# A transformer block in float32: the order of the down projection, where its weight sums are made, and the order of the up projection's matmuls

## The chip, the cores and the metric

The kernel runs on one core of one Trainium2 chip. The metric is the device time of one execution, in microseconds (us). Engines: TensorE (PE, with its weight loads as PEld), VectorE (DVE), ScalarE (ACT), GpSimd (POOL) and SyncE (SP, which here issues most loads). Each engine has a list of instructions of its own, in the order that the program gives; between engines semaphores decide.

## The reference

One block over 256 rows of 2048 columns: three kinds of attention, gates, an output product, and then the part that the change touches, a gated feed-forward layer with a short convolution.

```python
def reference(x, mem, ..., g_ffn, w_up, conv_w, conv_b, w_down):
    ...
        x = x + merged @ w_out[l]

        h2 = rms_norm(x, g_ffn[l])
        u = causal_depthwise_conv(h2 @ w_up[l], conv_w[l], conv_b[l])
        u_gate, u_val = jnp.split(u, 2, axis=-1)
        x = x + (jax.nn.silu(u_gate) * u_val) @ w_down[l]
    return x
```

`w_up` is 2048 x 11264, `w_down` 5632 x 2048.

## The kernel before

Products in float32 are made of parts. A piece of weights (128 partitions x 1024 columns, 512 KB) is loaded into `raw`; ACT rounds it to `hi`, DVE makes `lo = raw - hi`. The activations are kept as such parts too, and a product is two or three matmuls: in the down stage always three (`three`, L898): hi by hi, hi by the activation's lo, lo by hi. So each piece costs a load, one ACT and one DVE instruction ahead of its matmuls. `hi` and `lo` have four buffers each. `raw` has four in one pool and four more (`more`) in a pool that opens in the down stage; from the seventh load on they alternate (`buffer`, L874).

**Up stage** (L794 on). For 11 blocks of four row tiles of `u` and both halves (gate and value), 22 groups in all, it goes over eight pieces of `w_up`. Each piece holds two k tiles by four row tiles, and for each of these eight PE makes one long matmul (512 columns, L811: the weights' hi with both parts of the activations) and one short one (256 columns, L812: the weights' lo with the hi part). Long and short alternate. At five of the 22 groups (`BEATS`) a matmul of 32 columns on zeros goes ahead (L800). After each group the convolution (`conv`, L730) of its two row pairs follows on ACT and DVE: a copy `cr` out of PSUM, an add, a multiplication `u`, taps `y` and `z` on ACT with adds on DVE, and in the second half the product and its parts `aT`.

Beside it the up stage makes sums of down weights (`weight_sums`, L760): it loads four blocks of `w_down` into `r`, adds them on DVE and stores them by POOL's queue in DRAM tiles `T`, for the first half of the output columns in two stores, for the second half in one.

**Down stage** (L823 on). The output is made in two halves of 1024 columns, each in 22 products over two k tiles. `PLANS` has a letter for each. An `e` (`eight`, L911) takes two pieces and 24 long matmuls into four banks `X`. An `s` (`seven`, L926) gets the same result from seven block products, 21 matmuls, by sums of weight blocks (`t13`, `t42`) and sums of activation blocks (`forms`, L849), into `X` and four more banks `Y`, which `gather` (L954) adds up later. In the first half both sums of an `s` are loaded from `T`; in the second half `t13` is made here by two adds on DVE (L937, L938). The forms of product p are written some products ahead.

In this stage the instructions are written in a plain order, and the scheduler is free to move those of SP, ACT and DVE, by its own estimate of when things are due. Only instructions given to `keep_in_program_order` stay as written; in the down stage none are.

Of the kernel before, what the change touches and what calls it, by code (L numbers as in the profile page):

```python
# [44 lines left out]
def hybrid_block(  # L45
# [714 lines left out]
    def weight_sums(nb, p):  # L760
        n0 = nb * PIECE
        r = cps[2].tile([P, 2, 2, 512], F32, tag="r", name=f"r_{nb}_{p}")
        for j, n in ((0, 1), (0, 0), (1, 1), (1, 0)):
            tc.keep_in_program_order(
                nc.sync.dma_start(r[:, j, n], dv[:, 2 * p + j, n0 + n * 512 : n0 + (n + 1) * 512])
            )
            yield 1
        yield 1
        b01 = r[:, 0, 1]
        tc.keep_in_program_order(nc.vector.tensor_tensor(r[:, 0, 0], r[:, 0, 0], b01, ALU.add))  # L770
        if nb == 0:
# [4 lines left out]
        T = dram.tile([P, 2, 1024], F32, name=f"T_{nb}_{p}")  # L776
        made[nb, p] = T
        for h in range(nb, 2):
            yield 2
            nc.gpsimd.dma_start(T[:, h], r[:, h].rearrange("p b n -> p (b n)"))  # L780

# [12 lines left out]
    for f0 in range(0, FT, 4):  # L794
        for s in range(2):
            pairs = [two_banks(f"u{f0 + i}_{s}") for i in (0, 2)]
            c0 = s * D_FF + f0 * P
            if f0 // 2 + s in BEATS:
                tc.keep_in_program_order(
                    nc.tensor.matmul(pairs[0][:, 0, :32], lhsT=idle[:, :P], rhs=idle[:, :32], start=True, stop=True)  # L800
                )
            if asked and f0 // 2 + s > 0:
                adding.append([weight_sums(*asked.pop(0)), 0])
            for k in range(0, KT, 2):
                hi, lo = piece(upv[:, k : k + 2, c0 : c0 + 512], 2, 512, f"u{f0}_{s}_{k}")
                for j in range(2):
                    first, last = k + j == 0, k + j == KT - 1
                    for i in range(4):
                        c = slice(i * P, (i + 1) * P)
                        ps = pairs[i // 2][:, i % 2]  # L810
                        nc.tensor.matmul(ps, lhsT=hi[:, j, c], rhs=hT[:, k + j, :], start=first, stop=False)  # L811
                        nc.tensor.matmul(ps[:, :S], lhsT=lo[:, j, c], rhs=hT[:, k + j, :S], start=False, stop=last)  # L812
                add_on()
                tick()
# [16 lines left out]

    ov = out[0].rearrange("(t p) d -> p t d", p=P)
# [16 lines left out]
    def forms(p):  # L849
# [8 lines left out]
        nc.vector.tensor_tensor(  # L858
            d, two, v[:, 0, :, 1].unsqueeze(1).to_broadcast([P, 2, 2, P]), ALU.subtract
        )  # L860
        nc.vector.tensor_tensor(g, v[:, :, 0, 0], v[:, :, 1, 0], ALU.add)
        nc.vector.tensor_tensor(r[:, :2], d[:, :, 0], d[:, :, 1], ALU.add)
        nc.vector.scalar_tensor_tensor(r[:, FS2], r[:, FS1], -1.0, g[:, 0], ALU.mult, ALU.subtract)
        nc.vector.tensor_tensor(r[:, FS4], r[:, FS2], g[:, 1], ALU.add)
        to = sf[:, p] if p < 10 else form_of(p, slice(0, 3))
        last = form_of(p, FS4)
        nc.scalar.copy(to[:, :, 0], r[:, :3])
        nc.scalar.copy(last[:, 0], r[:, FS4])
        nc.vector.tensor_tensor(to[:, :, 1], r[:, :3], to[:, :, 0].bitcast(F32), ALU.subtract)
        nc.vector.tensor_tensor(last[:, 1], r[:, FS4], last[:, 0].bitcast(F32), ALU.subtract)  # L870
# [14 lines left out]
    def load_sums(T, h, name):  # L885
        t = buffer(f"raw_t{h}_{name}")
        nc.sync.dma_start(t, T[:, h])
        return t

    def parts(src, name):  # L890
# [3 lines left out]
        nc.scalar.copy(hi[:, :n], src)  # L894
        nc.vector.tensor_tensor(lo[:, :n], src, hi[:, :n].bitcast(F32), ALU.subtract)  # L895
# [14 lines left out]

    def eight(p, n0, X, first, last):  # L911
        w = []
        for k in (2 * p, 2 * p + 1):
            w.append(parts(load(k, n0), f"d{n0}_{k}"))
            if not last:
                for t in range(NT):
                    for n in range(2):
                        three(X[t][n], *a_of(k, t), w[-1][n], first and k == 2 * p)
            tick()
        if last:  # L920
            for t in range(NT):
                for n in range(2):
                    for j in range(2):
                        three(X[t][n], *a_of(2 * p + j, t), w[j][n], last=j == 1)

    def seven(p, n0, X, Y, first, last):  # L926
        k0, k1 = 2 * p, 2 * p + 1
        T = made[n0 // PIECE, p]
        full = n0 > 0
        raw0, raw1 = load(k0, n0, PIECE if full else 512), load(k1, n0)  # L930
        t13 = buffer(f"t13_{n0}_{p}") if full else load_sums(T, 0, f"{n0}_{p}")
        t42 = load_sums(T, 1, f"{n0}_{p}")
        (B00,) = parts(raw0[:, :512], f"d{n0}_{k0}")
        three(Y[0], *a_of(k0, 0), B00, first, last)
        B10, B11 = parts(raw1, f"d{n0}_{k1}")
        if full:
            nc.vector.tensor_tensor(t13[:, :512], raw0[:, :512], raw0[:, 512:], ALU.add)  # L937
            nc.vector.tensor_tensor(t13[:, 512:], raw0[:, 512:], raw1[:, 512:], ALU.add)  # L938
        three(X[0][0], *a_of(k1, 0), B10)
        three(X[0][1], *f_of(p, FS4), B11)  # L940
        tick()
        T1, T3 = parts(t13, f"t13_{n0}_{p}")
        three(Y[2], *f_of(p, FS1), T1, first, last)
        three(Y[3], *f_of(p, FS3), T3, first, last)
        T4, T2 = parts(t42, f"t42_{n0}_{p}")
        three(Y[1], *f_of(p, FS2), T2, first, last)
        three(X[1][0], *a_of(k1, 1), T4)
        tick()

    def gather(n0, Y):  # L950

        yield 3
        xr = lambda t, n: xrows[t, n]
        e, f = (sm.tile([P, 512], F32, tag="junk", bufs=2, name=f"{c}_{n0}") for c in "ef")  # L954
        nc.scalar.copy(e, Y[0])
        nc.vector.tensor_tensor(xr(0, 0), xr(0, 0), Y[0], ALU.add)
        nc.vector.tensor_tensor(e, e, Y[1], ALU.add)
        yield
        nc.vector.tensor_tensor(f, e, Y[2], ALU.add)
        nc.vector.tensor_tensor(e, e, Y[3], ALU.add)  # L960
        nc.vector.tensor_tensor(xr(0, 1), xr(0, 1), f, ALU.subtract)
        yield
        nc.vector.tensor_tensor(xr(1, 0), xr(1, 0), e, ALU.add)
        nc.vector.tensor_tensor(e, e, Y[2], ALU.add)
        nc.vector.tensor_tensor(xr(1, 1), xr(1, 1), e, ALU.subtract)

    formed = 0
    for nb, plan in enumerate(PLANS):
        n0 = nb * PIECE
        xrows = {}  # L970
        banks = [two_banks(f"d{nb}_{i}") for i in range(4)]
        if nb:
            banks = banks[2:] + banks[:2]
        X = [[banks[t][:, n] for n in range(2)] for t in range(NT)]
        Y = [banks[2 + i // 2][:, i % 2] for i in range(4)]
        ns, s = plan.count("s"), 0
        straight = list(range(FT // 2 - 1, ns - 1, -1)) if nb else list(range(ns, FT // 2))
        done = []
        for i, c in enumerate(plan):
            if c == "s":  # L980
                seven(s, n0, X, Y, s == 0, s == ns - 1)
                s += 1
                if s == ns:
                    later(gather(n0, Y))
            else:
                p = straight.pop(0)
                eight(p, n0, X, i == 0, i == len(plan) - 1)
                done.append(p)
                if len(done) == 4:
                    for t in range(NT):  # L990
                        for n in range(2):
                            xrows[t, n] = down_pool().tile([P, 512], F32, tag="xr", name=f"xr_{nb}_{t}_{n}")
                            nc.gpsimd.dma_start(xrows[t, n], xkeep[2 * nb + n][:, t])
                if formed < NSEVEN[0] and len(done) >= 2 or nb and formed < ns and len(done) > 1:
                    forms(formed)
                    formed += 1
        assert s == ns and not straight
        finish()
        for t in range(NT):
            for n in range(2):  # L1000
                o = sm.tile([P, 512], F32, tag="junk", bufs=2, name=f"o_{nb}_{t}_{n}")
                parts_ = 2 if (nb, t, n) == (1, 1, 1) else 1
                for i in range(parts_):
                    w = 512 // parts_
                    oc = slice(i * w, (i + 1) * w)
                    xc = slice(n0 + n * 512 + i * w, n0 + n * 512 + (i + 1) * w)
                    nc.vector.tensor_tensor(o[:, oc], xrows[t, n][:, oc], X[t][n][:, oc], ALU.add)
                    nc.scalar.dma_start(ov[:, t, xc], o[:, oc])

# [30 lines left out]
```

## Time and profile before

| | us |
|---|---|
| median of three runs (1508.73 to 1511.41) | 1509.15 |
| the profiled execution | 1509.21 |
| its span, first to last instruction | 1507.5 |
| L812, 1408 short matmuls of the up stage: busy, mean ns of one | 395.6, 281 |
| lo parts of `d` pieces, 128x1024, down stage (68): mean ns | 1219 |
| hi parts of the same: mean ns | 1051 |
| `raw_d` loads of 512 KB: median from issue to landing | 4.9 |
| `T` stores of 512 KB: median from issue to landing | 7.3 |

A matmul's record lasts longer than the spacing of two matmuls, because they are pipelined: 395 ns for a long one and 281 for a short one say little of the rate. The rate is read from starts, or from how many stand in a stretch. The up stage lies between 765.0 and 1261.1 us of the span, the down stage from there to 1501.3, and the rest is the last results and their stores.

### The profile page before, as it was taken

To read this page: it belongs to the slowest core of one execution; us is meant where nothing else is said; L and a number is where in the kernel's file an instruction comes from. 1 tells how busy PE (TensorE), PEld (TensorE's weight loads), DVE (VectorE), ACT (ScalarE), POOL (GpSimd) and SP (SyncE) were. 2 spreads that over 40 slices of the span, in tenths; PEclk is the share of its full clock that TensorE was granted. 3 is DMA by queue.
4 is the path that set the end of the run, shared out by engine and by line. 5 is a ranking of instruction groups with operands and counts; after the bars stand their busy time and mean duration, and the time that the engine had idled before them with its cause. 6 is when DMAs were issued, how large, how long until landed. Compare 5 with 4: busy or idle time off the path is not lost.

```text
span 1507.5 us, 20214 instructions
## 1 busy us (share of the span) xinstructions
PE 1489.7 (99%) x7410; PEld 1253.8 (83%) x7410; DVE 1038.4 (69%) x1331; ACT 864.6 (57%) x1227; POOL 38.8 (3%) x87
## 2 busy tenths in 40 slices
PE   9999999999999999999999999999999999999998
PEld 6888888888888888888888888888888887888776
DVE  5766566555655656565557788788778877978767
ACT  6755454358444444444557667667767766665543
POOL 0000000001000000000000000000000000000000
PEclk9999999999999999999999999999999999999999
DMA  8675475474666667656677887887787786888774
GB/s 299 197 204 160 126 219 163 114 228 147 190 201 208 192 202 200 191 188 202 216 224 237 280 287 262 288 299 255 244 278 239 252 252 209 299 291 272 241 231 150
DMA packets 159633, 336.87 MB, mean 223 GB/s; under 512 B 11674, under 2 KB 20526, under 8 KB 159534
## 3 DMA queue, kind: packets, MB, share of 16 engines
q1 hardware_dynamic: 152814, 314.08, 66.5%
q0 software_dynamic: 5392, 19.40, 3.4%
q10 hardware_dynamic: 1328, 2.11, 0.4%
q8 instruction: 58, 0.95, 0.3%
q14 instruction: 41, 0.34, 0.1%
HBM read 316.14 MB, written 19.40 MB: 223 GB/s over the span
## 4 chain that ended last, share of the span: by engine, by line
PE 87%; DMA 5%; DVE 4%; ACT 2%; issue 1%; POOL 0%; SPq 0%; DVEq 0%; ACTq 0%; POOLq 0%
PE u L811 19%; PE u L812 10%; PE g L158 5%; PE g L160 5%; PE g L159 5%; PE d L901 4%; PE d L899 4%; PE d L900 3%; PE s L158 2%; PE s L160 2%; PE f L160 2%; PE f L158 2%; PE f L159 2%; PE s L159 2%; DMA raw_d<-in_w_down_dram 2%; PE b L158 2%
## 5 line engine op out<-in xcount | busy, mean ns | idle before, releaser
L811 PE MATMUL u<-hT,hi_u 128*128 128x512 f32 x1408 | 493.7, 395 | 0.1
L812 PE MATMUL u<-hT,lo_u 128*128 128x256 f32 x1408 | 395.6, 281 | 0.3 <-DVE lo_u L148 0.2
L811 PEld LDWEIGHTS u<-hT,hi_u 128*128 128x128 f32 x1408 | 264.3, 188 | 61.3 <-issue 0.5
L148 DVE TENSOR_TENSOR lo_u<-raw_u,hi_u 128x1024 fp32r<-128x1024 f32 x176 | 213.5, 1221 | 80.3 <-ACT hi_u L147 80.3
L812 PEld LDWEIGHTS u<-hT,lo_u 128*128 128x128 f32 x1408 | 266.3, 189 | 2.3 <-DVE lo_u L148 2.2
L147 ACT CAST hi_u<-raw_u 128x1024 fp32r<-128x1024 f32 x176 | 182.5, 1047 | 124.2 <-PE u L811 63.0
L148 DVE TENSOR_TENSOR lo_g<-raw_g,hi_g 128x1024 fp32r<-128x1024 f32 x96 | 117.7, 1228 | 101.4 <-ACT hi_g L147 99.2
L147 ACT CAST hi_g<-raw_g 128x1024 fp32r<-128x1024 f32 x96 | 100.8, 1052 | 121.8 <-PE g L159 97.5
L158 PE MATMUL g<-hi_g,xT 128*128 128x512 f32 x384 | 151.0, 393 | 0.0
L160 PE MATMUL g<-lo_g,xT 128*128 128x512 f32 x384 | 149.7, 390 | 0.0
L159 PE MATMUL g<-hi_g,xT 128*128 128x512 f32 x384 | 149.6, 390 | 0.0
L894 ACT CAST hi_d<-raw_d 128x1024 fp32r<-128x1024 f32 (+1 forms) x88 | 83.1, 953 | 40.3 <-PE d L900 32.5
L901 PE MATMUL d<-lo_d,aT 128*128 128x512 f32 x252 | 99.6, 395 | 3.1 <-DVE lo_d L895 3.1
L899 PE MATMUL d<-hi_d,aT 128*128 128x512 f32 x252 | 98.8, 392 | 1.7 <-ACT hi_d L894 1.7
L895 DVE TENSOR_TENSOR lo_d<-raw_d,hi_d 128x1024 fp32r<-128x1024 f32 (+1 forms) x88 | 93.6, 1098 | 7.6 <-ACT hi_d L894 7.5
L900 PE MATMUL d<-hi_d,aT 128*128 128x512 f32 x252 | 98.6, 391 | 0.0
L160 PEld LDWEIGHTS g<-lo_g,xT 128*128 128x128 f32 x384 | 72.1, 188 | 15.3
L159 PEld LDWEIGHTS g<-hi_g,xT 128*128 128x128 f32 x384 | 72.2, 188 | 14.5
L158 PEld LDWEIGHTS g<-hi_g,xT 128*128 128x128 f32 x384 | 72.2, 188 | 14.5
L744 DVE TENSOR_TENSOR y<-y,z 128x512 f32<-128x512 f32 x88 | 60.7, 690 | 22.8 <-ACT z L743 19.7
L743 ACT ACTIVATE z<-u,taps 128x256 f32<-128x256 f32 x176 | 74.6, 496 | 0.0
L148 DVE TENSOR_TENSOR lo_s<-raw_s,hi_s 128x1024 fp32r<-128x1024 f32 (+1 forms) x40 | 44.7, 1118 | 37.2 <-ACT hi_s L147 37.1
(318 smaller groups left out, 2649.8 us busy)
## 6 DMA issues: line engine op xcount, KB each, us to landing
raw_u<-in_w_up_dram SPq DMA_DIRECT2D x176, 512.0 KB, 5.3
raw_g<-in_w_in_dram SPq DMA_DIRECT2D x96, 512.0 KB, 3.9
raw_d<-in_w_down_dram SPq DMA_DIRECT2D x79, 512.0 KB, 4.9
r<-in_w_down_dram SPq DMA_DIRECT2D x80, 256.0 KB, 6.7
raw_f<-in_w_in_dram SPq DMA_DIRECT2D x32, 512.0 KB, 3.6
raw_s<-in_w_in_dram SPq DMA_DIRECT2D x32, 512.0 KB, 3.6
raw_o<-in_w_out_dram SPq DMA_DIRECT2D x32, 512.0 KB, 4.8
T<-r POOLq DMA_DIRECT2D x29, 512.0 KB, 7.3
```

The lines of the kernel that those rows point to most:

```text
L147: pin(nc.scalar.copy(hi[:, :m], raw[:, :m]))
L148: pin(nc.vector.tensor_tensor(lo[:, :m], raw[:, :m], hi[:, :m].bitcast(F32), ALU.subtract))
L158: nc.tensor.matmul(o, lhsT=xh, rhs=wh, start=first, stop=False)
L159: nc.tensor.matmul(o, lhsT=xl, rhs=wh, start=False, stop=False)
L160: nc.tensor.matmul(o, lhsT=xh, rhs=wl, start=False, stop=last)
L811: nc.tensor.matmul(ps, lhsT=hi[:, j, c], rhs=hT[:, k + j, :], start=first, stop=False)
L812: nc.tensor.matmul(ps[:, :S], lhsT=lo[:, j, c], rhs=hT[:, k + j, :S], start=False, stop=last)
L894: nc.scalar.copy(hi[:, :n], src)
L895: nc.vector.tensor_tensor(lo[:, :n], src, hi[:, :n].bitcast(F32), ALU.subtract)
L899: nc.tensor.matmul(o, lhsT=ah, rhs=w[0], start=first, stop=False)
L900: nc.tensor.matmul(o, lhsT=al, rhs=w[0], start=False, stop=False)
L901: nc.tensor.matmul(o, lhsT=ah, rhs=w[1], start=False, stop=last)
```

## The change

1. **Down stage, order.** `eight` and `seven` no longer issue anything; they append steps, each a pair of functions: one that loads and makes parts, one that multiplies. A loop goes over all steps of both halves and makes the parts of step i + 2 (`AHEAD`) before the matmuls of step i. Every load, part, form, sum and result is kept in program order. An `e` is two steps, an `s` four.
2. **Forms** are now queued work (`later`): the first part (five instructions on DVE, two casts on ACT) is written after the matmuls of one step, the remainders after those of the next.
3. **Sums.** `t13` is made on DVE in both halves, from pieces loaded whole. `weight_sums` drops one add and one of two stores for the first half.
4. **Plan.** The first half has 14 `e` and 8 `s` (before 13 and 9), and opens with four `e`.
5. **Up stage.** For each k tile: long 0, long 1, short 0, short 1, long 2, long 3, short 2, short 3. The zeros are gone.

```diff
-PLANS = ("eee" + "se" * 8 + "see", "e" + "se" * 4 + "sse" + "se" * 3 + "ssee")
+PLANS = ("eeee" + "se" * 8 + "ee", "e" + "se" * 4 + "sse" + "se" * 3 + "ssee")
+AHEAD = 2
...
-BEATS = (2, 6, 10, 14, 18)
...
-        if nb == 0:
-            tc.keep_in_program_order(nc.vector.tensor_tensor(b01, b01, r[:, 1, 1], ALU.add))
...
-            if f0 // 2 + s in BEATS:
-                tc.keep_in_program_order(
-                    nc.tensor.matmul(pairs[0][:, 0, :32], lhsT=idle[:, :P], rhs=idle[:, :32], start=True, stop=True)
-                )
...
-                    for i in range(4):
+                    for i, part in ((0, hi), (1, hi), (0, lo), (1, lo), (2, hi), (3, hi), (2, lo), (3, lo)):
+                        ps = pairs[i // 2][:, i % 2]
                         c = slice(i * P, (i + 1) * P)
...
-    def load(k, n0, n=PIECE):
-        raw = buffer(f"raw_d{n0}_{k}")
-        nc.sync.dma_start(raw[:, :n], dv[:, k, n0 : n0 + n])
-        return raw[:, :n]
...
+    def load(src, name):
+        raw = buffer(f"raw_{name}")
+        keep(nc.sync.dma_start(raw, src))
+        return raw
...
+        def p2():
+            raw[2] = load(made[n0 // PIECE, p], f"t{name}")
+            raw[3] = buffer(f"t13_{name}")
+            keep(nc.vector.tensor_tensor(raw[3][:, :512], raw[0][:, :512], raw[0][:, 512:], ALU.add))
+            keep(nc.vector.tensor_tensor(raw[3][:, 512:], raw[0][:, 512:], raw[1][:, 512:], ALU.add))
+            w["T4"], w["T2"] = parts(raw[2], f"t42_{name}")
+
+        def p3():
+            w["T1"], w["T3"] = parts(raw[3], f"t13_{name}")
...
+                if formed < ns and n_done >= 2:
+                    at(len(steps) - 2, lambda p=formed: later(forms(p)))
+                    formed += 1
...
+    for prep, _ in steps[:AHEAD]:
+        prep()
+    for i, (_, use) in enumerate(steps):
+        if i + AHEAD < len(steps):
+            steps[i + AHEAD][0]()
+        use()
+        todo = after_step.pop(i, [])
+        for f in todo:
+            f()
+        tick()
+    finish()
```

How this moves the instructions is seen at two places. The first is ACT where the up stage ends: `cr_40_1` to `aT` are the last convolution, `hi_d0_21` (before) and `hi_d0_19` (after) are the hi parts of the fourth piece of the down stage. Before:

```order
L734 COPY cr_40_1_11148<-u40_1_10914 128x512
L894 CAST hi_d0_21_11222<-raw_d0_21_11220 128x1024
L739 ACTIVATE y_40_1_11152<-u_6450,taps_113 128x256 x2
L743 ACTIVATE z1_40_1_11155<-u_6450,taps_113 128x256 x2
L743 ACTIVATE z0_40_1_11159<-u_6450,taps_113 128x256 x2
L734 COPY cr_42_1_11166<-u42_1_10915 128x512
L894 CAST hi_d0_22_11256<-raw_d0_22_11254 128x1024
L894 CAST hi_d0_23_11274<-raw_d0_23_11272 128x1024
L752 CAST aT_6226<-y_40_0_10943 128x2x256
```

And in the changed kernel:

```order
L734 COPY cr_40_1_11127<-u40_1_10882 128x512
L739 ACTIVATE y_40_1_11131<-u_6450,taps_113 128x256 x2
L743 ACTIVATE z1_40_1_11134<-u_6450,taps_113 128x256 x2
L743 ACTIVATE z0_40_1_11138<-u_6450,taps_113 128x256 x2
L734 COPY cr_42_1_11145<-u42_1_10883 128x512
L752 CAST aT_6226<-y_40_0_10910 128x2x256
L739 ACTIVATE y_42_1_11149<-u_6450,taps_113 128x256 x2
L743 ACTIVATE z1_42_1_11152<-u_6450,taps_113 128x256 x2
L743 ACTIVATE z0_42_1_11156<-u_6450,taps_113 128x256 x2
L752 CAST aT_6226<-y_42_0_10926 128x2x256
L885 CAST hi_d0_19_11165<-raw_d0_19_11163 128x1024
L885 CAST hi_d0_20_11183<-raw_d0_20_11181 128x1024
```

Before, the fourth piece's hi part stood behind the first copy of the convolution, and the fifth and sixth in its middle; now the fourth (which is the piece `d0_19`, since the first half begins at another product) stands behind the last cast of `aT`.

The second place is DVE in the first half of the down stage: `fd`, `rbc` and `fr` are the first part of a form, `sf` and `aT` its remainders, `t13` the plain sums, `lo` the lo parts. Before:

```order
L895 TENSOR_TENSOR lo_d0_2_11410<-raw_d0_2_11401,hi_d0_2_11409 128x512
L863 SCALAR_TENSOR_TENSOR fr_2_11391<-fr_2_11391,rbc_5529 128x128
L895 TENSOR_TENSOR lo_d0_3_11417<-raw_d0_3_11403,hi_d0_3_11416 128x1024
L864 TENSOR_TENSOR fr_2_11391<-fr_2_11391,rbc_5529 128x128
L869 TENSOR_TENSOR sf_11125<-fr_2_11391,sf_11125 128x3x128
L870 TENSOR_TENSOR aT_6226<-fr_2_11391,aT_6226 128x128
L895 TENSOR_TENSOR lo_t13_0_1_11427<-raw_t0_0_1_11405,hi_t13_0_1_11426 128x1024
L861 TENSOR_TENSOR rbc_5529<-aT_6226 128x256
L895 TENSOR_TENSOR lo_t42_0_1_11437<-raw_t1_0_1_11407,hi_t42_0_1_11436 128x1024
L895 TENSOR_TENSOR lo_d0_26_11449<-raw_d0_26_11446,hi_d0_26_11448 128x1024
L895 TENSOR_TENSOR lo_d0_27_11467<-raw_d0_27_11464,hi_d0_27_11466 128x1024
```

And in the changed kernel:

```order
L886 TENSOR_TENSOR lo_s0_2_11384<-raw_s0_2_11381,hi_s0_2_11383 128x512
L855 TENSOR_TENSOR fd_3_11399<-aT_6226 128x512
L856 TENSOR_TENSOR rbc_5529<-aT_6226 128x256
L857 TENSOR_TENSOR fr_3_11400<-fd_3_11399 128x256
L858 SCALAR_TENSOR_TENSOR fr_3_11400<-fr_3_11400,rbc_5529 128x128
L859 TENSOR_TENSOR fr_3_11400<-fr_3_11400,rbc_5529 128x128
L886 TENSOR_TENSOR lo_s0_3_11411<-raw_s0_3_11408,hi_s0_3_11410 128x1024
L865 TENSOR_TENSOR sf_11092<-fr_3_11400,sf_11092 128x3x128
L866 TENSOR_TENSOR aT_6226<-fr_3_11400,aT_6226 128x128
L947 TENSOR_TENSOR t13_0_1_11430<-raw_s0_2_11381 128x512
L948 TENSOR_TENSOR t13_0_1_11430<-raw_s0_2_11381,raw_s0_3_11408 128x512
L886 TENSOR_TENSOR lo_t42_0_1_11434<-raw_t0_1_11428,hi_t42_0_1_11433 128x1024
```

Before, a form's instructions stood one by one between lo parts, and `t13` had only its lo part here. Now the first five stand in one block, two lo parts of an `s` stand around it, and the two adds of `t13` follow.

On ACT the same place reads now:

```order
L885 CAST hi_s0_2_11383<-raw_s0_2_11381 128x512
L862 CAST sf_11092<-fr_3_11400 128x3x128
L863 CAST aT_6226<-fr_3_11400 128x128
L885 CAST hi_s0_3_11410<-raw_s0_3_11408 128x1024
L885 CAST hi_t42_0_1_11433<-raw_t0_1_11428 128x1024
L885 CAST hi_t13_0_1_11440<-t13_0_1_11430 128x1024
```

The hi part of the second piece of the `s` (`hi_s0_3`) stands behind the two casts of the form, which wait for the block on DVE.

More of the change, by code (lines that the diff above doesn't have):

```diff
@@ L909, in f_of, with make, prep, use @@
         return to[:, 0], to[:, 1]
+    steps = []
     def eight(p, n0, X, first, last):
[L912 to L915, printed above, removed]
+        w = {}
+        def make(k):
+            def prep():
+                w[k] = parts(load(dv[:, k, n0 : n0 + PIECE], f"d{n0}_{k}"), f"d{n0}_{k}")
+            return prep
+        def use(k):
+            def run():
                 for t in range(NT):
                     for n in range(2):
-                        three(X[t][n], *a_of(k, t), w[-1][n], first and k == 2 * p)
-            tick()
@@ L926, in seven @@
+        steps.append((make(k0), (lambda: None) if last else use(k0)))
+        steps.append((make(k1), close if last else use(k1)))
     def seven(p, n0, X, Y, first, last):
         k0, k1 = 2 * p, 2 * p + 1
[L928 to L957, printed above, removed]
+        name = f"{n0}_{p}"
@@ L967, in hybrid_block @@
[L967 to L971, printed above, removed]
-        if nb:
[L973 to L998, printed above, removed]
```

138 lines of the change are left out of this document (103 added, 35 removed).

## The prediction

> **What bounds the kernel now.** I read the page's busy line first, then the groups, then stretches of the run with their counts of matmuls, then the chain and the rows around the places where TensorE (PE) waits.
>
> ```profile
> PE 1489.7 (99%) x7410; PEld 1253.8 (83%) x7410; DVE 1038.4 (69%) x1331; ACT 864.6 (57%) x1227; POOL 38.8 (3%) x87
> L811 PE MATMUL u<-hT,hi_u 128*128 128x512 f32 x1408 | 493.7, 395 | 0.1
> 1014.00:1172.00 158.00, 158.00 (x448) 84.07 (x447) 1.00 0.78 260
> 1172.00:1261.00 89.00, 89.00 (x258) 47.94 (x257) 1.00 0.73 236
> 1261.00:1287.00 26.00, 24.05 (x99) 0.93 0.72 242
> 1287.00:1381.00 94.00, 94.00 (x416) 1.00 0.85 288
> 1381.00:1500.00 119.00, 112.99 (x482) 0.99 0.66 218
> ```
>
> PE has a matmul under way nearly always, so what counts is how far apart matmuls start. The last five rows give it (stretch, length, busy time with the count in brackets, clock, DMA). The first two count L811 alone, that is, pairs of one long (512 columns) and one short (256) matmul of the up stage. A record that straddles an edge is counted too, so I take one fewer: 158/447 = 0.3535 us a pair in the first stretch, 89/257 = 0.3463 in the second. The same instructions run at two spacings, wide and close, 7.2 ns a pair apart. The 1408 pairs take 765.0 to 1261.1, 496.1 us, or 0.3523 each: between the two, with some waits.
>
> The last three rows are the down stage. Where nothing waits, 94/415 = 0.2265 us a long matmul. The first stretch then holds 98 x 0.2265 = 22.2 of 26 us, the last 481 x 0.2265 = 108.9 of 119. So the down stage loses 3.8 us at its start and 10.1 in its second half: 996 matmuls are 225.6 us and take some 240.
>
> ```profile
> 1279.21 0.50 PE L899 MATMUL d<-hi_d,aT 128*128 128x512 f32 x1 [1.50 <-ACT hi_d L894]
> 1438.30 0.80 PE L901 MATMUL d<-lo_d,aT 128*128 128x512 f32 x1 [2.92 <-DVE lo_d L895]
> 1430.58 5.75 DMA raw_d<-in_w_down_dram
> 1437.03 1.23 DVE lo_d L895
> DVE t L937 <- DMA raw_d<-in_w_down_dram: 20.8, 6, 4.1
> ```
>
> The two PE rows are the longest waits (in brackets); the next two are the chain to the second of them: a load whose buffer came free late, then its lo part, then PE. The last row, from the list of waits, is why buffers are late: VectorE (DVE) stood 20.8 us in six places at the add t (L937), which was placed ahead of lo parts that PE needed sooner and waited for a load of a later product.
>
> **The up stage.** The change keeps all 2816 matmuls and puts them long, long, short, short. No row shows that order. These show a run of shorts, each with weights of its own:
>
> ```profile
> 298.81 0.28 PE L159 MATMUL s<-hi_s,xT 128*128 128x256 f32 x1
> 298.93 0.28 PE L160 MATMUL s<-lo_s,xT 128*128 128x256 f32 x1
> 299.05 0.28 PE L158 MATMUL s<-hi_s,xT 128*128 128x256 f32 x1
> ```
>
> Short to short is 0.12, more than half of 0.2265. I read that as the next weights' load, which a short one is too short to cover. A close pair is then 0.2265 + 0.12 = 0.3465 (0.3463 above), and four in the new order 2 x 0.2265 + 2 x 0.12 = 0.693, the same as two close pairs. So the order gains nothing over the close spacing; it can gain by holding it. Bounds for the stage: all close 1408 x 0.3463 = 487.6, all wide 497.7. I add 2.5 for the start and odd waits (it now loses about 3 beside the spacings), and take the close end, since the run of shorts shows 0.12 each time: 490.1, **6.0 us less**. The other end, 500.2, is 4.1 more. The five zeros cost 0.2 us at most (five matmuls of 32 columns) and lie in this sum. Twelve of 69 adds of weight sums and ten of 29 stores of 512 KB also leave the stage, off PE's path; they speak for fewer odd waits and are in the 2.5.
>
> The Trainium skill ("TensorE: Matmul & The Clock Gate", "LDWEIGHTS (loading the stationary operand)") gives a weight load as columns / 1.2, so 107 ns for 128 columns, and says that the queue pulls weight loads ahead of running matmuls. By that a short one, 0.113, would cover its load. The 0.12 above speaks against it; what it would make of the time is a rival below.
>
> **The down stage, matmuls.** One product of seven becomes one of eight: 999 for 996, 226.3 us, +0.7.
>
> **The down stage, its start.** ScalarE (ACT) and DVE now take the fourth piece's parts after the whole convolution of the last two row pairs; before, such parts stood inside it.
>
> ```profile
> 1260.69 0.59 ACT L734 COPY cr<-u 128x512 f32<-128x512 f32 x1 [1.15 <-PE u L812]
> 1261.27 1.06 ACT L894 CAST hi_d<-raw_d 128x1024 fp32r<-128x1024 f32 x1
> 1265.47 0.59 ACT L734 COPY cr<-u 128x512 f32<-128x512 f32 x1
> 1266.11 0.68 DVE L735 TENSOR_TENSOR cr<-cr,u 128x512 f32<-128x512 f32 x1
> 1266.70 0.68 DVE L750 TENSOR_TENSOR y<-y,y 128x512 f32<-128x512 f32 x1
> 1267.31 0.69 DVE L736 TENSOR_TENSOR u<-cr,rbc 128x512 f32<-128x512 f32 x1
> 1269.37 1.70 ACT L743 ACTIVATE z<-u,taps 128x256 f32<-128x256 f32 x4
> 1273.83 0.62 ACT L752 CAST aT<-y 128x512 fp32r<-128x512 f32 x1 [2.77 <-DVE y L750]
> ```
>
> Without what lay between: second cr at 1265.5 as now, u done 1268.0, y and z 1.0 + 1.7 to 1270.8, an add and L750 at 0.7 each to 1272.2, the cast of aT to 1272.8, then hi of the fourth piece 1.05 to 1273.9 and its lo to 1275.1. PE has three pieces ready, 36 matmuls or 8.2 us, to 1269.4. It waits **4.5 us**, where before it went on.
>
> **The down stage, first half: forms and sums on DVE.** Spacing from a dense stretch (start, duration, engine, line):
>
> ```profile
> 1300.24 0.42 DVE L861 TENSOR_TENSOR rbc<-aT 128x256 f32<-128x256 f32 x1
> 1300.57 0.42 DVE L862 TENSOR_TENSOR fr<-fd 128x256 f32<-128x256 f32 x1
> 1300.91 1.22 DVE L895 TENSOR_TENSOR lo_t<-raw_t,hi_t 128x1024 fp32r<-128x1024 f32 x1
> 1302.04 0.28 DVE L863 SCALAR_TENSOR_TENSOR fr<-fr,rbc 128x128 f32<-128x128 f32 x1
> 1302.24 0.68 DVE L858 TENSOR_TENSOR fd<-aT 128x512 f32<-128x512 f32 x1
> 1302.85 0.28 DVE L864 TENSOR_TENSOR fr<-fr,rbc 128x128 f32<-128x128 f32 x1
> 1307.06 0.55 DVE L869 TENSOR_TENSOR sf<-fr,sf 128x384 fp32r<-128x384 f32 x1
> 1307.53 0.28 DVE L870 TENSOR_TENSOR aT<-fr,aT 128x128 fp32r<-128x128 f32 x1
> 1307.73 1.82 DVE L895 TENSOR_TENSOR lo_d<-raw_d,hi_d 128x512 fp32r<-128x512 f32 x2
> 1391.88 0.52 ACT L867 CAST sf<-fr 128x384 fp32r<-128x384 f32 x1 [0.72 <-DVE fr L863]
> 1392.69 0.30 ACT L868 CAST aT<-fr 128x128 fp32r<-128x128 f32 x1 [0.29 <-DVE fr L864]
> 1393.00 1.05 ACT L894 CAST hi_t<-t 128x1024 fp32r<-128x1024 f32 x1
> ```
>
> Start to start, 1024 columns take 1.14, 512 take 0.6, 256 0.33, 128 0.2, the sf remainder 0.47. Before, the scheduler strewed a form's instructions among lo parts. Now its first five stand together, and the next piece's hi stands on ACT behind the form's two casts. DVE's next lo therefore starts after 0.60 + 0.33 + 0.45 + 0.30 (fd, rbc, fr and L863, with 0.1 for results that the next needs at once) + 0.52 + 0.2 + 1.05 = 3.4 us from the form's start, in which DVE works 1.9. A product of seven with one of eight, with a form, is for DVE 0.6 (lo, 512) + 3.4 + 1.14 + 0.67 (the form's remainders) + 1.2 (two plain sums, before made in the up stage) + 4 x 1.14 = **11.6 us**; for PE it is 45 x 0.2265 = 10.2. Before it was 5 x 1.14 + 0.6 + some 2.5 for the form = 8.8, under 10.2, which is why 1287 to 1381 shows no wait. Now DVE is the bound while forms last: eight in the first half, three in the opening products of eight and five in pairs.
>
> From the lo parts of pieces four and five, done at 1276.3: forms 0 and 1 with what stands behind them 6.4 + 5.8, form 2 to the T parts of the first pair 7.6, then five pairs of 11.6, to 1354.1. PE needs that part after 96 + 225 + 11 = 332 matmuls, 75.2 us from 1261.3: 1336.5. It is **17.6 us late**, the 4.5 among them, against 3.8 before. What could hide this is four hi and lo buffers, three pieces of lead; but DVE starts without lead, from the wait before it. If all the same the forms hid, 4.5 and some 1.4 us at a lower clock would be left (0.93 in the first stretch above): 5.9. The upper end is 20, with stalls at each pair's DMAs. I take 17.6, worked from the order of the queues.
>
> **Second half.** The fixed order has each add behind the lo parts of its own two loads, so the add no longer stands in front of something needed; each load waits for a buffer eight back, some 8 to 12 us of PE time ahead, against 5.75 + 1.05 + 1.22 of load, hi and lo. The 10.1 us go. Three forms stand here, 3 x 1.4 = 4.2 less about 1.7 of lead that the pairs without forms rebuild: 2.5 back (0 to 5). Results and tail keep their instructions.
>
> **The sum**, on the profiled execution's 1509.2 (span 1507.5), 0.06 from the median of 1509.15: up -6.0; down 226.3 + 17.6 + 2.5 = 246.4 against some 240 (225.6 + 3.8 + 10.1): +6.5, the 0.7 in it. **1510 us**: a gain and a loss of one size.
>
> **Rivals.** A row of the last of the five zeros:
>
> ```profile
> 1172.31 0.19 PE L800 MATMUL u<-idle 128*128 128x32 bf16 x1
> ```
>
> **Wide spacing kept:** at this zero the wide stretch ends and the close one begins, so a zero can shift the spacing. Without them a wide one, if the new order has one, can hold. In half the stage the up stage gains some 1 us: 1515. In all of it, 7.2 ns x 1408 above the close case: 1520, slower; it decides, that is, passes 1512, once over a quarter of the pairs run wide. For: 158 us above at one spacing. Against: 0.12 in runs of shorts. **DVE keeps up:** forms hide under the lead and only 5.9 is lost: down 232.2, 7.8 less than now, 1496; with half hidden, 1503. For: DVE 69% busy, no wait in the first half now. Against: the 11.6. **Loads hidden:** two longs let both loads of the shorts come early, four matmuls in 0.68: 704 x 0.68 = 478.5, 15 less in the up stage: 1501. 0.12 speaks against it. The Trainium skill's rule above would give this case.
>
> **How the numbers follow.** My case 0.45 (its own range 1505 to 1515); wide in half 0.15, in all 0.13; DVE keeps up 0.20; loads hidden 0.07. Within 0.2% is 1506 to 1512, about what a measurement of this kernel can tell from none. My case gives 0.08 faster, 0.27 same, 0.10 slower; the wide cases 0.04 same, 0.24 slower; the last two 0.26 faster, 0.01 same. Together 0.34, 0.32, 0.34. The range 1497 to 1518 leaves out about a fifth.
>
> **What would show it.** Pairs of starts in the up stage at 0.693 for four throughout; a wait of PE of 4 to 5 us near the eighth microsecond of the down stage, released by the fourth piece's hi; then waits of about 1.4 us for lo parts, once a pair, through six pairs, with DVE waiting for ACT behind each form; none at the add t. It would be wrong if four matmuls take another time than 0.693, if the conv's end doesn't hold the fourth piece, or if PE runs through the form pairs unheld.

## The result, and the profile after

| | before | after |
|---|---|---|
| median, us (4 runs each) | 1508.94 (1506.82 to 1511.41) | 1517.57 (1517.38 to 1517.83) |
| ratio after to before | | 1.0057 (1.0039 to 1.0074) |
| up stage, first to last start | 765.02 to 1261.07 | 765.14 to 1256.68 |
| down stage, from there to the last start | 240.0 | 252.6 |

The change made the kernel slower by 8.6 us. Between the profiled executions the up stage gives 4.5 us, the down stage takes 12.5, and the results behind it 0.3. The forecast was 1510, inside it 490.1 for the up stage (it took 491.5) and 246.4 for the down stage.

From the page of the changed kernel: the busy line, the group of the up stage's long matmuls and that of the first of the three matmuls with a `d` piece in the down stage, with the idle time ahead of them.

```profile
PE 1489.3 (98%) x7408; PEld 1250.9 (83%) x7408; DVE 1044.5 (69%) x1333; ACT 859.6 (57%) x1225; POOL 33.6 (2%) x77
L805 PE MATMUL u<-hT,hi_u 128*128 128x512 f32 x1408 | 442.4, 396 | 0.1
L890 PE MATMUL d<-hi_d,aT 128*128 128x512 f32 x200 | 79.2, 396 | 4.3 <-ACT hi_d L885 4.3
```

The shares hardly tell the kernels apart; the stretches do. Stretch, length, then busy time (and count) of PE, PEld, DVE, ACT and POOL, granted clock, DMA share, GB/s. The first row counts L805 alone (PE and PEld), in the middle of the up stage; the others are the down stage.

```profile
1014.00:1172.00 158.00, 142.43 (x455) 69.10 (x454) 1.00 0.78 258
1257.00:1290.00 33.00, 27.65 (x109) 21.21 (x107) 24.14 (x42) 16.50 (x29) 2.19 (x4) 0.90 0.53 175
1291.00:1356.00 65.00, 58.80 (x251) 45.91 (x252) 57.32 (x83) 35.45 (x46) 0.00 (x0) 1.00 0.70 227
1358.00:1388.00 30.00, 30.00 (x134) 24.84 (x133) 24.59 (x27) 15.23 (x16) 0.56 (x2) 1.00 0.81 279
1389.00:1445.00 56.00, 50.96 (x212) 39.61 (x211) 44.17 (x61) 27.80 (x35) 1.10 (x2) 0.97 0.72 225
1445.00:1508.00 63.00, 63.00 (x280) 52.18 (x279) 53.28 (x59) 34.15 (x37) 0.00 (x0) 1.00 0.67 222
```

Up stage: 454 longs in 158 us, two to a four of long, long, short, short: 158/227 = 0.696 us a four. Taking all starts, each group of 32 fours from the second to the last but one takes 22.29 us, 0.697 a four: one spacing, no waits.

Down stage: PE is full wherever no forms are made (1358 to 1388, 1445 to 1508) and is not where they are. The list of PE's waits (total, times, longest), and two rows of the lists of ACT and DVE:

```profile
PE d L890 <- ACT hi_t L885: 10.2, 10, 1.2
PE d L890 <- ACT hi_d L885: 4.3, 1, 4.3
PE d L890 <- ACT hi_s L885: 2.7, 2, 1.9
ACT hi_s L885 <- DVE o L1016: 11.3, 1, 11.3
DVE o L1016 <- DMA out_dram<-o: 8.3, 3, 4.7
```

Here is one pair with a form (start, duration, engine, line; idle time before and its releaser in brackets), DVE, then ACT:

```profile
1295.57 0.69 DVE L855 TENSOR_TENSOR fd<-aT 128x512 f32<-128x512 f32 x1
1297.29 0.29 DVE L859 TENSOR_TENSOR fr<-fr,rbc 128x128 f32<-128x128 f32 x1
1298.98 1.23 DVE L886 TENSOR_TENSOR lo_s<-raw_s,hi_s 128x1024 fp32r<-128x1024 f32 x1 [1.40 <-PE d L891]
1297.28 0.51 ACT L862 CAST sf<-fr 128x384 fp32r<-128x384 f32 x1 [3.34 <-DVE fr L858]
1297.90 1.04 ACT L885 CAST hi_s<-raw_s 128x1024 fp32r<-128x1024 f32 x1
```

ACT is idle for 3.3 us until the form is there; then come the casts; then `hi_s`; only then DVE's `lo_s`, which starts 3.4 us after the form (1295.57 to 1298.98), as the forecast had it. DVE idles 1.4 us in that. The releaser named, PE, had long been done; it was `hi_s`. A pair with a form then takes 11.7 us from start to start, five in a row behind a first of 13.4; one without takes 10.2.

The place that the forecast lacked is the boundary of the halves:

```profile
1386.41 1.28 DVE L1016 TENSOR_TENSOR o<-xr,d 128x512 f32<-128x512 f32 x2
1392.44 0.69 DVE L1016 TENSOR_TENSOR o<-xr,d 128x512 f32<-128x512 f32 x1 [4.75 <-DMA out_dram<-o]
1394.53 0.69 DVE L1016 TENSOR_TENSOR o<-xr,d 128x512 f32<-128x512 f32 x1 [1.40 <-DMA out_dram<-o]
1387.12 8.47 ACTq L1017 DMA_DIRECT2D out_dram<-o  x4
1395.71 1.57 ACT L885 CAST hi_s<-raw_s 128x512 fp32r<-128x512 f32 x2 [11.28 <-DVE o L1016]
1396.38 0.50 PE L890 MATMUL d<-hi_s,aT 128*128 128x512 f32 x1 [1.93 <-ACT hi_s L885]
```

The third result on DVE waits 4.75 us for the store of the first, since results have two buffers. ACT issues the stores, in order, over 8.5 us, and the next piece's hi stands behind the last one. PE runs dry. In the kernel before, these stores stood between the hi parts of the next pieces, and the hi part behind the last of them waited 0.60 us, not 11.28 (ACT):

```profile
1383.36 0.34 ACTq L1008 DMA_DIRECT2D out_dram<-o  x1
1384.47 1.05 ACT L894 CAST hi_t<-raw_t 128x1024 fp32r<-128x1024 f32 x1 [1.67 <-PE d L900]
1385.69 0.34 ACTq L1008 DMA_DIRECT2D out_dram<-o  x1
1386.13 2.52 ACT L894 CAST hi_d<-raw_d 128x1024 fp32r<-128x1024 f32 x3 [0.60 <-DVE o L1007]
```

Two of PE's waits, the one at the start of the stage and the one at the boundary, cost more than their length. Around the end of the first and behind the second the granted clock is 0.50 (rows as in the table of stretches), and there matmuls start 0.43 us apart:

```profile
1267.50:1274.30 6.80, 4.85 (x11) 3.36 (x12) 5.17 (x9) 3.43 (x6) 2.19 (x4) 0.50 0.82 253
1397.20:1400.60 3.40, 3.40 (x8) 2.37 (x9) 3.29 (x4) 1.77 (x3) 0.00 (x0) 0.50 0.30 97
```

A start is late by what its distance from the start before it exceeds 0.2265 us. Adding up all that are over 0.06 us late in the down stage: at the start 4.45 of waiting and 2.6 of matmuls at half clock; at the forms of the first half 10.1; at the boundary 2.1 and 2.1; at the three forms of the second half 3.9. Together 25.2.

### The profile page after: what moved, and what is told of

Same layout as the page of the kernel before. It is cut to its first block, busy times and chain, and to the rows that moved or that the text cites. A ratio compares the mean times of both kernels' runs of the same rounds, so it can differ in the third digit from the quotient of the medians.

```text
span 1515.9 us, 20136 instructions
## 1 busy us (share of the span) xinstructions
PE 1489.3 (98%) x7408; PEld 1250.9 (83%) x7408; DVE 1044.5 (69%) x1333; ACT 859.6 (57%) x1225; POOL 33.6 (2%) x77
## 4 chain that ended last, share of the span: by engine, by line
PE 92%; ACT 3%; DVE 2%; issue 1%; DMA 1%; POOL 0%; ACTq 0%; DVEq 0%; SPq 0%; POOLq 0%
PE u L805 22%; PE u L807 11%; PE g L158 5%; PE g L160 5%; PE g L159 5%; PE d L890 4%; PE d L892 4%; PE d L891 4%; PE s L158 2%; PE s L160 2%; PE s L159 2%; PE f L158 2%; PE f L160 2%; PE f L159 2%; PE b L158 2%; PE b L160 2%
## 5 line engine op out<-in xcount | busy, mean ns | idle before, releaser
L805 PE MATMUL u<-hT,hi_u 128*128 128x512 f32 x1408 | 442.4, 396 | 0.1
L807 PEld LDWEIGHTS u<-hT,lo_u 128*128 128x128 f32 x1408 | 264.5, 188 | 62.5
L807 PE MATMUL u<-hT,lo_u 128*128 128x256 f32 x1408 | 276.6, 278 | 0.0
L805 PEld LDWEIGHTS u<-hT,hi_u 128*128 128x128 f32 x1408 | 214.3, 189 | 0.5 <-issue 0.5
L890 PE MATMUL d<-hi_d,aT 128*128 128x512 f32 x200 | 79.2, 396 | 4.3 <-ACT hi_d L885 4.3
L892 PE MATMUL d<-lo_d,aT 128*128 128x512 f32 x200 | 78.7, 394 | 0.0
L891 PE MATMUL d<-hi_d,aT 128*128 128x512 f32 x200 | 78.6, 393 | 0.0
L148 DVE TENSOR_TENSOR lo_f<-raw_f,hi_f 128x1024 fp32r<-128x1024 f32 (+1 forms) x40 | 44.7, 1119 | 34.5 <-ACT hi_f L147 33.0
L147 ACT CAST hi_f<-raw_f 128x1024 fp32r<-128x1024 f32 (+1 forms) x40 | 38.6, 967 | 52.3 <-PE f L159 47.6
```

Of the source, the lines that this page charges most:

```text
L147: pin(nc.scalar.copy(hi[:, :m], raw[:, :m]))
L148: pin(nc.vector.tensor_tensor(lo[:, :m], raw[:, :m], hi[:, :m].bitcast(F32), ALU.subtract))
L890: nc.tensor.matmul(o, lhsT=ah, rhs=w[0], start=first, stop=False)
L891: nc.tensor.matmul(o, lhsT=al, rhs=w[0], start=False, stop=False)
L892: nc.tensor.matmul(o, lhsT=ah, rhs=w[1], start=False, stop=last)
```

## The experiments

All times are medians; ratios are to the kernel before on the same chip, with their 95% intervals. The changed kernel's 1517.57 is the other point of comparison; since the medians of the kernel before lie between 1508.2 and 1510.4 from chip to chip, a difference from it is good to a microsecond or two.

### The up stage's edits alone, in the kernel before

```diff
-            if f0 // 2 + s in BEATS:
-                ...
-                    for i in range(4):
+                    for i, part in ((0, hi), (1, hi), (0, lo), (1, lo), (2, hi), (3, hi), (2, lo), (3, lo)):
```

> The kernel before, with the up stage's two edits alone: long, long, short, short, and no zeros; the down stage and the weight sums stay as before. If the gain of the up stage is its own (one spacing of 0.697 us for four matmuls throughout, in place of two spacings), the stage is 4.4 us shorter as in the changed kernel and the time 1504.5. Rival: the gain came from the twelve adds and ten stores that also left the up stage; then the stage is at most 2 us shorter and the time 1507 or more.

Measured: 1506.58 (1501.76 to 1510.32), ratio 0.9989 (0.9979 to 1.0000). L808 is the long matmul here:

```profile
1014.00:1172.00 158.00, 142.56 (x455) 69.04 (x454) 1.00 0.80 269
```

The spacing is that of the changed kernel, 158/227 = 0.696. But the stage takes 493.0 us, since three groups (the eighth, ninth and eleventh) are 0.3 to 0.65 longer than 22.29. So in this profile 3 us of the 4.5 come from the two edits, and 1.4 were lost again in waits that the changed kernel, with fewer sums in this stage, does not have. Neither the theory (4.4 us) nor the rival (2 at most) is met whole. The gain of the median is smaller still, 1.7, and hardly outside its interval.

### The zeros alone taken out of the kernel before

```diff
-            if f0 // 2 + s in BEATS:
-                ...
```

> The kernel before, without its five zeros and nothing else (order long, short, long, short). If the zeros move the up stage from its wide spacing to its close one, the stage without them keeps one spacing from group 1 on (22.19 or 22.62 us a group of 128 matmuls), and the time is 3 us less or 3 to 4 more; if something else moves it (waits between pieces), both spacings are seen again and the time is that of before within 2 us.

Measured: 1509.81 (1501.27 to 1512.32), ratio 0.9997 (0.9983 to 1.0012). Rows for the short matmul, L807:

```profile
790.00:830.00 40.00, 39.81 (x116) 21.53 (x115) 1.00 0.71 235
1014.00:1172.00 158.00, 158.00 (x448) 84.02 (x448) 1.00 0.78 260
1172.00:1256.00 84.00, 84.00 (x239) 44.67 (x238) 1.00 0.73 233
```

The stage begins close (39.8/115 = 0.346 a pair), is wide in its middle (158/447 = 0.3535) and stays so to its end (84/238 = 0.353), where the kernel before went back to the close spacing at a zero. It turned in its fifth group, in which there is a wait; the third group has one too (22.44 us, where 22.19 is close) without that effect. The stage is 1.3 us longer than before, so the gain of the run above is not that of leaving out the zeros. Both expectations are half right: something beside the zeros moves it one way, and in this run nothing moved it back. The starts of the kernel before show that a zero has no fixed effect: at the zeros of the seventh and eleventh groups the spacing goes from close to wide, at that of the nineteenth from wide to close, at the other two it stays. Small events without a zero move it there too, to wide in the fourth group and back to close in the fifth. In the new order all twelve profiles have 22.29 in every undisturbed group.

### The results added in place

```diff
-                o = sm.tile([P, 512], F32, tag="junk", bufs=2, name=f"o_{nb}_{t}_{n}")
+                o = xrows[nb, t, n]
```

> The changed kernel, with the results added in place in the residual's tile and stored from there, so that no result waits for a buffer of the result before it. Theory: after the half's end the third result stands for 4.7 us on DVE for the store of the first, ACT's store issues stand behind it and the next piece's hi behind them; that is PE's wait of 2.1 us at the second product of the second half, and the slower matmuls right behind it (2.1 us more): 4.2 less, 1513.4. Rival: the second half is bound by its forms all the same and the wait comes back at the next pair: 1516 to 1517.6.

Measured: 1512.21, ratio 1.0024 (1.0015 to 1.0033), 5.4 less than the changed kernel.

```profile
1386.51 1.28 DVE L1016 TENSOR_TENSOR xr<-xr,d 128x512 f32<-128x512 f32 x2
1389.14 1.28 DVE L1016 TENSOR_TENSOR xr<-xr,d 128x512 f32<-128x512 f32 x2 [1.35 <-PE d L892]
```

The third add now waits for PE's last matmuls of the half only, and PE has no wait at the boundary. 4.2 us are that; 0.6 come from the first form behind it, which now delays PE by 0.5 in place of 1.1, and 0.7 from the last results, which end sooner after the last matmul (5.95 us in place of 6.64).

### Four pieces ahead of the last convolution

```diff
-    for prep, _ in steps[:AHEAD]:
+    for prep, _ in steps[:4]:
...
-        if i + AHEAD < len(steps):
+        if 4 <= i + AHEAD < len(steps):
```

> The changed kernel, with four pieces made ready ahead of the last convolution in place of three. Theory A (waits add): PE's first wait of 4.5 us and the 2.6 us of slower matmuls behind it go, 7.0 less, 1510.5. Theory B (DVE is the bound until the forms end; what PE doesn't wait at the start it waits at the form pairs): DVE ends its forms no sooner than by one lo part, 1.1, and the waits come back at the pairs, 1515 to 1517.

Measured: 1516.56, ratio 1.0056 (1.0043 to 1.0069). Theory B. PE's waits:

```profile
PE d L890 <- ACT hi_t L885: 8.4, 10, 1.2
PE d L890 <- ACT hi_s L885: 3.4, 2, 2.1
PE d L890 <- ACT hi_d L885: 1.8, 2, 1.6
```

The wait of 4.3 for `hi_d` is gone, and 1.8 for `hi_d` and more for `hi_s` stand in its place: the late starts of the first half go from 17.1 to 16.2 us. The wait at the start is real, but it isn't a cost that can be taken away by itself: DVE sets when the forms are done.

### The forms' casts one step later

```diff
         keep(nc.vector.scalar_tensor_tensor(r[:, FS2], ...))
         keep(tt(r[:, FS4], r[:, FS2], g[:, 1], ALU.add))
+        yield
         keep(nc.scalar.copy(to[:, :, 0], r[:, :3]))
...
-                    at(len(steps) - 2, lambda p=formed: later(forms(p)))
+                    at(len(steps) - 3, lambda p=formed: later(forms(p)))
```

> The changed kernel, with each form begun one step earlier and its two casts on ACT put one step behind its DVE part, so that the next piece's hi no longer stands on ACT behind casts that wait for DVE. Theory A (the order of the queues: DVE idles some 1.2 us behind each form because ACT's hi stands behind the form's casts): the waits of 1.3 to 1.4 us a pair go, 5 x 1.4 + 3.1 in the first half and 3.9 in the second, 14.0 less, 1503.6; DVE's own work, 10.5 us a pair against PE's 10.2, gives back 2 at most. Theory B (DVE's work is the bound, through the plain sums): the pairs stay above 11 us and the time above 1512.

Measured: 1509.88, ratio 1.0009 (1.0001 to 1.0018): 7.7 less, half of what A promised. The pairs take 11.1. On DVE:

```profile
1316.52 0.29 DVE L859 TENSOR_TENSOR fr<-fr,rbc 128x128 f32<-128x128 f32 x1
1316.73 0.69 DVE L887 TENSOR_TENSOR lo_s<-raw_s,hi_s 128x512 fp32r<-128x512 f32 x1
1318.21 1.23 DVE L887 TENSOR_TENSOR lo_s<-raw_s,hi_s 128x1024 fp32r<-128x1024 f32 x1 [0.80 <-ACT hi_s L886]
```

One short lo part (0.6) now stands between the form and the next hi that is made behind its casts; the casts and that hi take 1.7 on ACT. DVE still idles 0.8. This left open whether the rest was order or work.

### The forms two steps earlier

The same edit, with `at(len(steps) - (3 if formed < 3 else 4), ...)` and `yield 0 if p < 3 else 1` ahead of the casts.

> As the run with the form's casts one step later, but with the form begun two steps earlier (in the pairs; one step in the three opening products), so that two lo parts stand on DVE between the form and the next hi that ACT makes behind the casts. There ACT still stood behind DVE and DVE idled 0.9 us a pair. Theory: that idle time goes, DVE's work is 11.1 - 0.9 = 10.2 a pair, PE's own 10.2, and nine waits of 0.8 go: 1509.9 - 7 = 1503. Rival: the rest of the wait has another cause and the pairs stay at 11.1: 1509 to 1510.

Measured: 1503.71, ratio 0.9965 (0.9953 to 0.9978), as the theory had it. No pair waits, in either half:

```profile
1291.00:1353.00 62.00, 62.00 (x272) 50.29 (x271) 59.26 (x85) 37.27 (x47) 0.00 (x0) 1.00 0.79 267
```

DVE makes as many instructions as before in a pair, and is busy 59.3 of 62 us; PE doesn't wait. So the idle time behind the casts was the cause. What is left of late starts is 7.5 at the start and 4.3 at the boundary.

### The plain sums loaded again

```diff
+        if nb == 0:
+            tc.keep_in_program_order(nc.vector.tensor_tensor(b01, b01, r[:, 1, 1], ALU.add))
...
+        for h in range(nb, 2):
+            yield 2
+            nc.gpsimd.dma_start(T[:, h], r[:, h].rearrange("p b n -> p (b n)"))
...
+            if n0 == 0:
+                raw[3] = load(made[0, p][:, 0], f"t13_{name}")
```

> The changed kernel, with the two plain sums of each first-half product of seven made in the up stage again and loaded (eight adds more and eight stores of 512 KB more there, eight loads more and sixteen adds fewer in the down stage). Theory A (DVE's chain of work and idle time sets the pairs while forms last): 1.2 us of adds fewer in each of six pairs, pair 11.7 to 10.5, 6 x 1.2 = 7.2 less: 1510.4. Rival (only the order behind the form's casts counts, DVE would stand idle that much longer): pairs stay at 11.7 and the time at 1516 to 1518.

Measured: 1511.02 (1509.24 to 1513.69), ratio 1.0014 (1.0005 to 1.0023), 6.6 less. Theory A.

```profile
1299.00:1353.00 54.00, 54.00 (x236) 43.61 (x235) 45.27 (x63) 32.62 (x42) 0.00 (x0) 1.00 0.91 303
```

Pairs take 10.4 us. Less work on DVE does as much as less idle time, since what counts is the sum of both: 10.3 of work and 1.4 of idle time are too much, and either part taken away brings the pair near PE's 10.2. The late starts of the first half fall by 7.9, to 9.1; the up stage got 2.2 longer, in its seventh to tenth groups.

### All of it, and with the opening forms later

All four edits (results in place, four pieces, forms two steps earlier, sums loaded):

> All of it together: results in place, forms begun two steps earlier with the casts behind, plain sums loaded, four pieces ahead of the last convolution. Theory (waits go at the start only once DVE has room to catch up): 5.3 for the results, 14 for the forms' waits, up to 6 at the start: 1494 with bounds 1491 to 1499. Rival (the start's wait comes back at the pairs whatever DVE has to do): 1500 or more.

Measured: **1496.97** (1496.45 to 1498.43), ratio 0.9923 (0.9911 to 0.9935).

```profile
1257.00:1285.00 28.00, 24.34 (x94) 19.31 (x93) 23.41 (x41) 16.01 (x29) 2.18 (x4) 0.88 0.67 232
1285.00:1488.00 203.00, 203.00 (x897) 168.15 (x896) 171.78 (x216) 115.68 (x133) 2.19 (x4) 1.00 0.77 264
```

From 1285 on PE never waits. 7.0 us are left at the start, two waits and the half clock behind them; the theory had expected 6 of the start to go, and only the bound of its range held:

```profile
1268.95 0.50 PE L894 MATMUL d<-hi_d,aT 128*128 128x512 f32 x1 [1.56 <-ACT hi_d L889]
1271.79 0.80 PE L896 MATMUL d<-lo_d,aT 128*128 128x512 f32 x1 [2.11 <-DVE lo_d L890]
```

Two runs were to win the second of these, where the first form stands ahead of that lo part, by beginning the three opening forms one step later.

> All of it together again, with the three opening forms begun one step later (as in the changed kernel), so that the fifth piece's lo stands on DVE ahead of the first form. With that form ahead of it PE waited 1.7 us for the fifth piece's hi and 2.3 for its lo. Theory: the second of these falls to what the lo alone takes behind its hi, 0.7: 1.6 less, and as much of the slow matmuls stays: 1495.4. Rival: the opening forms end later by as much and PE waits at the first pair instead: 1497.

> As the run before it, but with the plain sums made on DVE in the down stage, as in the changed kernel. DVE's work is then 10.2 us a pair, PE's 10.2. Theory (no room to catch up): what is gained at the start comes back at the pairs, 1498.5 (1503.7 of the run with the forms begun earlier, less 5.3 for the results). Rival (DVE has room all the same): 1495 to 1496.

Measured: 1500.00, ratio 0.9940 (0.9923 to 0.9957), and 1500.40, ratio 0.9942 (0.9925 to 0.9959). Both expectations missed. The waits moved to the fifth and sixth pieces and to the first pair, with half clock once more, 8.6 and 9.2 us in all against 7.0; the first of the two also has 2.4 us more in its up stage. After the first pair the second kernel, with the plain sums on DVE, runs like the other: its adds cost nothing once the order leaves no idle time.

```profile
1291.00:1485.00 194.00, 194.00 (x854) 159.41 (x854) 172.94 (x219) 112.69 (x132) 2.17 (x4) 1.00 0.77 260
```

### Parts made three pieces ahead, and two lines in all

```diff
-AHEAD = 2
+AHEAD = 3
```

> The changed kernel with AHEAD = 3 and nothing else. The adds of the plain sums then stand on DVE between a form and the next hi that ACT makes behind the form's casts, and fill 1.2 us of the idle time there. Theory A (DVE's work and idle time set the pairs): pairs 10.5 in place of 11.7, nine or ten times 1.2 less, the start's wait repaid but for 1: 1505. Theory B (what counts is the lead in pieces, and four buffers of hi and lo set it at either number): 1515 to 1518.

Measured: 1504.39, ratio 0.9973 (0.9961 to 0.9986). Theory A. On DVE:

```profile
1306.05 0.29 DVE L859 TENSOR_TENSOR fr<-fr,rbc 128x128 f32<-128x128 f32 x1
1306.26 0.69 DVE L947 TENSOR_TENSOR t<-raw_s 128x512 f32<-128x512 f32 x1
1306.86 0.68 DVE L948 TENSOR_TENSOR t<-raw_s,raw_s 128x512 f32<-128x512 f32 x1
1307.74 1.23 DVE L886 TENSOR_TENSOR lo_t<-raw_t,hi_t 128x1024 fp32r<-128x1024 f32 x1 [0.20 <-ACT hi_t L885]
```

The two adds, which need nothing of ACT, now stand where DVE idled 1.4 us; 0.2 is left, and the pairs take PE's 10.2. Not one instruction is fewer. With the results in place as well:

> AHEAD = 3 and the results added in place, no other edit. Theory: PE's wait at the half's boundary, 3.2 us, and the 2.0 us of slow matmuls behind it go: 1504.4 - 5.2 = 1499.2. Rival (the forms of the second half then have too little lead, since the wait gave it to them): 1501 or more.

Measured: 1499.27 (1498.57 to 1499.32), ratio 0.9930 (0.9917 to 0.9944).

```profile
1291.00:1490.00 199.00, 199.00 (x876) 164.17 (x875) 176.45 (x227) 110.53 (x129) 2.19 (x4) 1.00 0.75 249
```

Two lines turn the change from 0.6% slower into 0.7% faster. What is left is 9.0 us of late starts in the opening of the stage.

## Why the prediction was right and wrong

The time lies in the range, near its upper end, and 7.6 us over the forecast: a forecast of no change for a change that costs 0.6%. That it lies in the range is luck: the forecast's own case ended at 1515, and only the rivals with the wide spacing, which did not come, reached beyond that. Two slips in the sums change nothing: 704 x 0.68 is 478.7, and the bracket behind "some 240" adds up to 239.5.

- **Up stage, 490.1:** took 491.5. One spacing held, as forecast, and the rival of the wide spacing fell; so did that of hidden loads, 0.68 a four. Mis-sized: "four in the new order 2 x 0.2265 + 2 x 0.12 = 0.693" is 0.697, so that the stage at one spacing is 490.4 and not 487.6, 2.8 us more; the start and odd waits were 1.1 and not the 2.5 allowed. Its parts were off in a way that nearly cancels: the timeline of the changed kernel, two matmuls to a row, has 0.47 and 0.46 from two longs to the next row and 0.23 from two shorts, some 0.233 a long one and 0.116 a short.

```profile
1049.88 0.63 PE L805 MATMUL u<-hT,hi_u 128*128 128x512 f32 x2
1050.35 0.39 PE L807 MATMUL u<-hT,lo_u 128*128 128x256 f32 x2
1050.58 0.63 PE L805 MATMUL u<-hT,hi_u 128*128 128x512 f32 x2
1051.04 0.40 PE L807 MATMUL u<-hT,lo_u 128*128 128x256 f32 x2
```

  The 107 ns of the Trainium skill for a weight load ("TensorE: Matmul & The Clock Gate", "LDWEIGHTS (loading the stationary operand)") is an estimate by its rule, columns / 1.2. It lies 9 ns below these shorts, and the 0.12 lay 4 ns above them; the longs rose by as much as the shorts fell, so the 0.68 a four that the rival drew from that rule did not come.
- **Down stage's start, 4.5:** 4.45, at the place and with the releaser named. Behind it stood 2.6 of half clock, which the sum did not have. It made no difference, since the 17.6 was reckoned from DVE's chain; the run with four pieces showed that this chain is what holds.
- **First half, 17.6:** 17.9 (132.1 us for 504 matmuls of 0.2265). The pair of 11.6 is 11.7, the 3.4 behind a form is 3.4, and the opening forms take 6.35, 5.83 and 7.65 on DVE where the sum had 6.4, 5.8 and 7.6; so this term is no luck. The rival that DVE keeps up fell. Only the releaser differs: PE waits for the hi part of `t13`, made behind the adds, more than for a lo part. That both the work (the plain sums) and the idle time (the casts) carry it, each alone being enough, was shown by taking away either.
- **Second half, 2.5 back:** 8.4, and here is the step that failed. "Results and tail keep their instructions" is true of the instructions and says nothing of their order: the stores and the adds before them, which the scheduler had put between the parts of the next pieces, now all stand ahead of the next part. The results in place gave the 4.2 back, and 5.4 in the time. The forms took 3.9 and not 2.5: the three stand in three pairs that follow each other, where the first is 1.1 late and the others 1.4 each, so hardly any lead was there or was rebuilt between them.
- **None at the add t:** right. What the change was to remove it removed; it put a larger wait in its place.

So 1.4 in the up stage, 4.2 at the boundary, 1.4 at the last forms, 0.3 in the first half and 0.3 in odd places make up the difference.

## What to carry to other kernels

Where an order is fixed by the program, walk each in-order engine past every place that is not the steady loop (the end of a stage, the boundary of halves) and ask of each instruction that can wait what stands behind it: here a store that waited for a buffer held the next weights on ACT. In an alternation between two engines, put work that needs nothing of the other engine between the request and the answer; the same instructions in another order were worth 13 us. Before taking a wait away, ask whether another engine is the bound until later: the largest single wait, 4.5 us, gave back some 1 us, because DVE had the same work left.

## What the runs showed of the hardware

- The granted clock can go to half behind waits of PE as short as 2.1 us. Each time the trace has it at half for 3.41 or 6.83 us (the two rows above), with matmuls 0.43 us apart. In the changed kernel and its variants that followed eight of nine waits that made a start 2.1 to 2.3 us late, and cost about as much again as the wait; it followed a few of those of 1.4 to 1.75 us, and most of those below cost 0.1 beside their length. Length alone does not decide: in the run with the up stage's edits alone a start 3.3 us late (at 1436.9) was not followed by it, the clock staying at 1.00. The Trainium skill ("TensorE: Matmul & The Clock Gate", "Wait — 56ns, not 53.3ns?") gives 426.7 ns from start to start for 512 columns at the low clock, with which the 0.43 agrees.
- The same matmuls have two spacings in the old order (0.346 and 0.3535 us a pair), and change from one to the other at small events. Nearly all of the difference lies in the step from a long matmul to the short one behind it: in the kernel before 0.230 us in a close stretch and 0.237 in a wide one, while the step from short to long is 0.116 and 0.117. In the new order there was one spacing, in twelve profiles, with 0.233 a long one. Why is open. It was not tried what in the order decides it.
- With the larger number of sums in the up stage, three of four profiles in the new order have waits of 0.1 to 1 us in three or four of its groups (2.5 us together at most); with the smaller number, none of eight. The times of the kernels with the larger number spread by 2 to 9 us, those of the others by 0.4 to 1.7. Whether adds or stores cause it was not tried.
